# A hybrid RG-LRU and attention layer: the fourth column tile of xr takes block 0 of x with the first three, and the LRU work stands one step later

## Chip, core and metric

The kernel runs on one core of one Trainium2 chip. The metric is the device time of one execution in microseconds (us). Engines are named as in the profile: PE does the matmuls, PEld loads their weights, DVE is the vector engine, ACT the scalar engine, POOL is GpSimd, SP only issues DMAs here. L435 is line 435 of the kernel before the change.

## What is computed

One layer of an encoder trunk on x of 512 positions by 1024 channels, in float32:

```
h = RMSNorm(x)
[xr | gate | q | k | v] = h @ W_in                  # 512, 512, 512, 512, 512 columns
xr = depthwise conv of width 4 over positions
h_f, h_b = forward and backward RG-LRU of xr        # r, i = sigmoid gates of xr, block by block
y_rnn = (h_f + h_b) * gelu(gate)
y_attn = dilated attention of q, k, v, 8 heads, with a T5 bias by relative position
x = x + concat(RMSNorm(y_rnn), RMSNorm(y_attn)) @ W_out
x = x + relu(RMSNorm(x) @ W_up)^2 @ W_down
out = RMSNorm(x)
```

In the RG-LRU, a = exp(c r) and b = sqrt(1 - a^2) * i * xr feed a scan over the positions, one forward and one backward.

## The kernel before

**Precision.** Every float32 operand is split into two parts (hi on ACT by a copy to the matmul type, lo on DVE by subtracting hi), and each product is three matmuls: hi·hi, hi·lo and lo·hi, done by mm3 (L303 to L305). Weights come in chunks of 128x1024. For chunk i, conv_hi(i) makes whi (L251 on ACT, L249 on DVE for chunks 7, 8 and 9), and conv_lo(i) makes wlo on DVE (L259). conv_lo also issues the load of a later chunk into the buffer that it has read.

**Order.** PE, ACT, DVE and POOL run their instructions in the order in which the program's text emits them, so an instruction that waits holds all that stand behind it on its engine. DMAs issued by ACT (L468) and POOL stand in those orders too. SP issues the other DMAs.

**The head.** x comes transposed in eight blocks k of 128 channels; each comes with the 3x128 weight columns of column tiles 0 to 2 of xr for that block (L325 to L328). cvx(k) (L336) makes h_hi and h_lo of the block (x times the norm's gain; the row factor rstd is applied later) and splits its weights. sq(k) squares x for the norm. PE adds up pxr[0..2] over k as the blocks come (L431 to L438). Within the last block it also transposes the sum of squares (turned, L422, the tile pcs). From pcs come the row sums on DVE (L427), rcol on POOL (a power, L403), and by a PE transpose (prow, L395) and an ACT copy the tile rstd (rrow, L409). The fourth column tile pxr[3] uses chunk 3, a whole 128x1024 chunk loaded after the blocks, and is computed afterwards by xmm (L648), in pieces before and after prow.

**conv and LRU.** conv_a(t) multiplies pxr[t] by rstd (DVE L486) and starts the conv on ACT (L488). conv_b(t) adds its other three taps on DVE (L493 to L495). POOL meanwhile runs a softplus polynomial (L161 to L173, some twenty tiny operations) that starts from a DVE result emitted behind conv_a(1) (L159, L160) and whose last results scale the exponentials. Behind it POOL issues the load of the bias rows (relt, L664).

**V and gate.** The loop over 32 steps n for V (L695) makes one mm3 per step, about 0.68 us, and one over 32 steps of the gate projection follows (L734). Other work is hung on step numbers: GATES says at which n lru_gates(t) puts 8 small matmuls (pg, L514) and their sigmoids (ga, L517). lru_hooks(n) hands out lru_x (DVE L522), lru_exp (ACT L531, L532), lru_sqrt (ACT L537), and, at the numbers in SC, the 16 pieces of the scans (DVE L548, L549, L555, L557). bias_round(0) at n = 7 is the first user of relt on DVE (L454). bias_prep at n = 20 is two matmuls, two DVE negations (nbs, L467) and two DMAs issued by ACT (L468); it stands behind lru_hooks(20) in that step, so behind lru_exp(2) and the first scan piece.

**Into attention.** 16 steps of K and Q of head pair 0 follow. k_evac (kraw, L750) and q_evac (qraw, L746) read PSUM on DVE. s_hi (ACT L757) and s_lo (DVE L766 for K, L769 for Q) split the results, and att_s (PE L782, L783) forms the scores ps. A dictionary plan says which extra work stands at which point of the attention loop; rnn_end(t) is two DVE operations (L582, L583) that add the two scans and multiply by the gate, and rnn_end(0) stands at point (0, 0, 0), just after the first scores.

Of the kernel before, what the change touches and what calls it, by code (L numbers as in the profile page):

```python
# [14 lines left out]
AF = mybir.ActivationFunctionType  # L15
OP = mybir.AluOpType

P = 128
S = 512
D = 1024  # L20
KD = D // P
# [80 lines left out]
def hybrid_kernel(ctx: ExitStack, tc, xw0, xw, xn, w_in, w_v, w_out, w_up, w_dn, gates, vecs, rel, onehot, fg, out):  # L102
    nc = tc.nc
# [8 lines left out]
    act = nc.scalar.activation  # L112
# [3 lines left out]
    def g_(name, dt=FT, shape=(P, S)):  # L116
        return work.tile(list(shape), dt, name=name, tag="g", bufs=NG)
# [4 lines left out]
    def ps_(name, tag):  # L122
        return psum.tile([P, S], FT, name=name, tag=tag, bufs={"pj": 4, "gs": 2, "et": 2}[tag])

    def f(t):
        return t.bitcast(FT)
# [175 lines left out]
    def mm3(o, a, b, first, last, on=False):  # L302
        nc.tensor.matmul(o, lhsT=a[0], rhs=b[0], start=bool(first), stop=False, skip_group_check=on)  # L303
        nc.tensor.matmul(o, lhsT=a[0], rhs=b[1], start=False, stop=False, skip_group_check=on)  # L304
        nc.tensor.matmul(o, lhsT=a[1], rhs=b[0], start=False, stop=bool(last), skip_group_check=on)  # L305
# [13 lines left out]
    for k in range(KD):  # L319
        if 4 <= k < 7:  # L320
            xwt.append(stream.tile([P, 1024], FT, name="wraw", tag="wraw", bufs=3)[:, :XW])
        else:
            xwt.append(work.tile([P, 1024], FT, name="tw", tag="tw", bufs=4)[:, :XW if k else XG + 3 * P])
        if k == 0:
            nc.sync.dma_start(xwt[0][:, :XG], xw0[:, :XG])  # L325
            nc.sync.dma_start(xwt[0][:, XG:], xw0[:, XG:])
        else:
            nc.sync.dma_start(xwt[k], xw[k - 1])  # L328
        if k == 6:
            nc.sync.dma_start(vt, vecs)  # L330
# [5 lines left out]
    def cvx(k):  # L336
        x, w = xwt[k][:, :S], xwt[k][:, S if k else XG:]
        g = ag[:, k:k + 1] if k else xwt[0][:, S:S + 1]
        hi, lo = g_("w3h", FR), g_("w3l", FR)
        if k < 2:  # L340
            c = (2 * P, 3 * P)[k]
            act(h_hi[:, k, :c], x[:, :c], AF.Copy, scale=g)
            nc.vector.tensor_scalar(h_hi[:, k, c:], x[:, c:], g, None, op0=OP.mult)
            if k == 0:
                nc.vector.tensor_copy(hi[:, :2 * P], w[:, :2 * P])
                act(hi[:, 2 * P:3 * P], w[:, 2 * P:], AF.Copy)
            else:
                nc.vector.tensor_copy(hi[:, :3 * P], w)
        else:
            act(h_hi[:, k, :], x, AF.Copy, scale=g)  # L350
            act(hi[:, :3 * P], w, AF.Copy)
        stt(h_lo[:, k, :], x, g, f(h_hi)[:, k, :], op0=OP.mult, op1=OP.subtract)
        nc.vector.tensor_tensor(lo[:, :3 * P], w, f(hi)[:, :3 * P], op=OP.subtract)
        w3.append((hi, lo))

    def sq(k):
# [22 lines left out]
    def hk(k):  # L379
        return (h_hi[:, k, :], h_lo[:, k, :])  # L380

    def wk(c, k):
        if c < 3:
            return tuple(t[:, c * P:(c + 1) * P] for t in w3[k])
        hi, lo = splits[c]
        return (hi[:, k * P:(k + 1) * P], lo[:, k * P:(k + 1) * P])
# [19 lines left out]
    def row_tile(cols, tag):  # L406
        pr = rows_of(lambda tt: fan(cols, tt, 1, P), tag)
        r = g_("rrow")
        act(r, pr, AF.Copy)  # L409
        return r  # L410
# [8 lines left out]
    def turned(ss, tag):  # L419
        pc = ps_("pcs", tag)  # L420
        for tt in range(4):
            nc.tensor.transpose(pc[:, tt * P:(tt + 1) * P], ss[:, tt * P:(tt + 1) * P], ident)  # L422
        return pc
# [3 lines left out]
        nc.vector.tensor_reduce(c, pc.rearrange("p (t c) -> p t c", t=4), axis=mybir.AxisListType.X, op=OP.add)  # L427
        return c

    pxr = {t: ps_("pxr", "pj") for t in range(3)}  # L430
    for k in range(KD):  # L431
        if k < 2:
            for i, (a, b) in enumerate(((0, 0), (0, 1), (1, 0))):
                for t in range(3):
                    nc.tensor.matmul(pxr[t], lhsT=wk(t, k)[a], rhs=hk(k)[b], start=i == 0 and k == 0, stop=False)  # L435
            continue
        for t in range(3):
            mm3(pxr[t], wk(t, k), hk(k), False, k == KD - 1)  # L438
            if k == KD - 1 and t == 0:
                sqt = turned(sqx[0], "et")  # L440


# [41 lines left out]
    def conv_a(t, pp):  # L484
        xr = g_("xr")
        nc.vector.tensor_tensor(xr, pp, rstd, op=OP.mult)  # L486
        c = g_("xc")
        act(c, xr, AF.Identity, scale=vec("w2", t), bias=vec("cb", t))  # L488
        xrt[t], xc[t] = xr, c

    def conv_b(t):
        xr, c = xrt.pop(t), xc[t]
        stt(c[:, 2:], xr[:, :S - 2], vec("w0", t), c[:, 2:], op0=OP.mult, op1=OP.add)  # L493
        stt(c[:, 1:], xr[:, :S - 1], vec("w1", t), c[:, 1:], op0=OP.mult, op1=OP.add)
        stt(c[:, :S - 1], xr[:, 1:], vec("w3", t), c[:, :S - 1], op0=OP.mult, op1=OP.add)  # L495
        xcs[t] = swapped("xcs", c)
# [22 lines left out]
    def lru_x(t):  # L519
        for m, x in ((1, xc[t]), (3, xcs.pop(t))):  # L520
            o = gact[t, m]
            nc.vector.tensor_tensor(o, o, x, op=OP.mult)  # L522
        del gwr[t], xc[t]
# [3 lines left out]
    def lru_exp(t):  # L527
        for d in range(2):
            r = gact[t, 2 * d]
            a = g_("la")  # L530
            act(a, r, AF.Exp, scale=cneg[:, d * 4 + t:d * 4 + t + 1])  # L531
            act(r, r, AF.Tanh, scale=chalf[:, d * 4 + t:d * 4 + t + 1])  # L532
            lru_a[t, d] = a
# [5 lines left out]
    def lru_gelu(t):  # L539
        act(gt[t], gt[t], AF.Gelu_apprx_tanh)  # L540
# [102 lines left out]
                sub.popleft()()  # L643


    pxr[3] = ps_("pxr", "pj")

    def xmm(ks):  # L648
        for k in ks:
            mm3(pxr[3], wk(3, k), hk(k), k == 0, k == KD - 1)  # L650

    for i in (3, 4, 5):
        conv_hi(i)
# [1 line left out]
    rcol = rstd_cols(row_sums(sqt), D)  # L655
    for i in (4, 5):
        conv_lo(i)
    xmm((0, 1, 2))
    rstd = row_tile(rcol, "et")
    conv_a(0, pxr[0])  # L660
    conv_a(1, pxr[1])
# [2 lines left out]
    nc.gpsimd.dma_start(relt, rel)  # L664
    for i in range(2):
        nc.gpsimd.dma_start(oht[i], onehot[:, i * S:(i + 1) * S])
    xmm((3, 4))
    conv_b(0)
    act(warm, epsb, AF.Sigmoid)
    conv_a(2, pxr[2])  # L670
    xmm((5, 6, 7))
    conv_a(3, pxr[3])
    conv_hi(6)
    conv_b(1)
# [4 lines left out]
    def lru_hooks(n):  # L679
        if n in (9, 10, 13, 14):  # L680
            lru_x({9: 0, 10: 1, 13: 2, 14: 3}[n])
        if n in (13, 14, 20, 21):
            lru_exp({13: 0, 14: 1, 20: 2, 21: 3}[n])
        if n in (17, 19, 28, 29):
            t = {17: 0, 19: 1, 28: 2, 29: 3}[n]
            lru_sqrt(t)
            scans.extend(scan_ops(t)[:4])
        if n in SC:
            scans.popleft()()

    GATES = {2: 0, 5: 1, 8: 2, 11: 3}
    pv = {}
    vtag = {0: "et", 2: "gs", 3: "gs", 1: "et"}
    steps = [(k, tt) for k in range(KD) for tt in (0, 2, 3, 1)]
    for n, (k, tt) in enumerate(steps):  # L695
        c = C_V + k // 2
        if k == 0:
            pv[tt] = ps_("pv", vtag[tt])
        hi, lo = splits[c]
        sl = slice((k % 2) * S, (k % 2 + 1) * S)  # L700
        tsl = slice(tt * P, (tt + 1) * P)
        mm3(pv[tt], (h_hi[:, k, tsl], h_lo[:, k, tsl]), (hi[:, sl], lo[:, sl]), k == 0, k == KD - 1)
        if n >= 16:
            feed(c, n % 8)
        if n in GATES:
            lru_gates(GATES[n])
        if n == 2:
            conv_b(2)
        if n == 6:
            conv_b(3)  # L710
            conv_lo(6)
        if n == 7:
            conv_hi(7)
            conv_lo(7)
        if n in (7, 9):
            bias_round((n - 7) // 2)
        if n == 12:
            conv_hi(8)
            conv_lo(8)
        lru_hooks(n)  # L720
        if n == 20:
            bias_prep()
            load_tw(0)
            load_tw(1)
    vs = big.tile([P, 4, S], FT, name="vs", tag="bigC")
    last = [scan_ops_end(t) for t in range(4)]
# [6 lines left out]
    gsteps = [th for t in range(4) for th in proj_thunks(C_G + t, "pj", gate_done(t))]  # L733
    for n, th in enumerate(gsteps):  # L734
        th()
        lru_hooks(32 + n)
        if n in (19, 21, 27, 29):
            tt = {19: 0, 21: 2, 27: 3, 29: 1}[n]
            act(vs[:, tt, :], pv[tt], AF.Copy, scale=rcol[:, tt:tt + 1])
# [191 lines left out]
    def wo_thunks():  # L931
# [17 lines left out]
            return run  # L949
        return [mk(b, *o) for b, o in enumerate(order)]  # L950

    KSPLIT = {7: s_hi, 8: s_lo}
    for n, th in enumerate(q_thunks(0, 1) + q_thunks(0, 0)):
        th()
        if n in KSPLIT:
            for e in range(2):
                KSPLIT[n](0, 1, e)
        if n % 4 == 0:
            lru_gelu(n // 4)
    fillers = deque()  # L960

    def fill(n):
# [22 lines left out]
            for b in bs[1:]:  # L985
                nc.gpsimd.dma_start(t, oblock(b), accum_op=OP.add)

    def rnn_end(t):
        last[t]()

    def rnn_sq(t):
        y_sq(yrnn[t], 0)

# [6 lines left out]
    def end(t):  # L1000
        return lambda: rnn_end(t)

    def sq_(t):
        return lambda: rnn_sq(t)
# [4 lines left out]
    def op(fn, *a):  # L1009
        return lambda: fn(*a)  # L1010


    plan = {(0, 0, 0): [end(0)], (0, 0, 2): [sq_(0), add], (0, 0, 3): [end(1)],
            (0, 1, 1): [sq_(1)],
            (0, 2, 3): [add],
            (1, 0, 2): [end(2)],
# [138 lines left out]
    for w in OSEQ:  # L1155
        for i in range(4):
            tt, k = i // 2, i % 2
# [550 lines left out]
```

## Time and profile before

| | |
|---|---|
| median of 3 runs | 540.1 us (539.34 to 540.29) |
| the profiled execution, its own time | 539.75 us |
| its span, first to last instruction | 538.0 us |
| time around the span | 1.75 us |
| granted PE clock, mean | 0.997 |
| instructions | 8174 |

The profile shows one execution. A row of its timeline gives start and duration in us, the engine and line, output <- inputs, a shape, how many instructions are merged (x2), and in brackets how long the engine had been idle before and what ended that. A merged row's duration covers all its instructions; neighbours overlap by about 0.1 us, since an engine starts the next instruction while the last one drains. A matmul row of 0.39 us is one of a pipelined stream in which the next starts 0.23 us later. PE and DVE rows are therefore compared by their starts.

### The profile page before, as it was taken

What the parts mean: (1) busy time and instruction counts of PE and PEld (TensorE: products, weight loads), DVE (VectorE), ACT (ScalarE), POOL (GpSimd) and SP (SyncE); (2) the same over time, 40 slices, a digit from 0 to 9 for tenths busy, and PEclk for the clock granted to TensorE, in tenths of its full rate; (3) what the DMA queues carried; (4) which work ended last, traced back from release to release, by engine and by line L of the source; (5) the groups of instructions that cost most, each with busy time, mean ns of one, the idle gap of its engine ahead of it and who ended that gap; (6) DMA issues with size and microseconds to landing.
All of it is one profiled execution on the core that took longest, in us unless ns stands there. A gap on an engine that the chain in (4) does not pass through costs nothing.

```text
span 538.0 us, 8174 instructions
## 1 busy us (share of the span) xinstructions
PE 530.2 (99%) x3007; PEld 450.3 (84%) x3007; DVE 433.7 (81%) x636; ACT 362.3 (67%) x574; POOL 67.5 (13%) x92
## 2 busy tenths in 40 slices
PE   9999999999999999999999999999999999999995
PEld 7857888886886578889999888888999999888884
DVE  6895998996863689889769987879756987987885
ACT  6678955898865746586566755566657686755664
POOL 0182000000001131001030223001101210131000
PEclk9999999999999999999999999999999999999998
DMA  7743385465499788856586799994887496799704
GB/s 276 246 110 109 111 274 185 130 184 158 117 361 239 163 161 231 285 188 176 175 171 179 193 252 275 288 358 115 282 236 200 130 218 185 173 290 262 190 1 157
DMA packets 36664, 108.00 MB, mean 201 GB/s; under 512 B 4484, under 2 KB 7556, under 8 KB 36624
## 3 DMA queue, kind: packets, MB, share of 16 engines
q1 hardware_dynamic: 28480, 78.49, 42.5%
q0 software_dynamic: 7968, 28.76, 28.5%
q8 instruction: 23, 0.38, 0.3%
q10 hardware_dynamic: 176, 0.23, 0.1%
q14 instruction: 17, 0.14, 0.1%
HBM read 98.00 MB, written 4.23 MB: 190 GB/s over the span
## 4 chain that ended last, share of the span: by engine, by line
PE 98%; DVE 0%; issue 0%; DVEq 0%; ACT 0%; ACTq 0%
PE pu L303 10%; PE pu L305 10%; PE pu L304 10%; PE pd L305 9%; PE pd L303 9%; PE pd L304 9%; PE pqk L303 3%; PE pwo L303 3%; PE pqk L304 3%; PE pqk L305 3%; PE pav L897 3%; PE pt L806 3%; PE pwo L305 3%; PE pwo L304 3%; PE pv L303 2%; PE pp L305 1%
## 5 line engine op out<-in xcount | busy, mean ns | idle before, releaser
L259 DVE TENSOR_TENSOR wlo<-wraw,whi 128x1024 fp32r<-128x1024 f32 x73 | 88.9, 1220 | 20.5 <-ACT whi L251 20.2
L251 ACT ACTIVATE whi<-wraw 128x1024 fp32r<-128x1024 f32 x70 | 74.1, 1060 | 36.2 <-PE pd L305 18.8
L304 PE MATMUL pd<-wlo,ah 128*128 128x512 f32 (+1 forms) x195 | 75.2, 386 | 0.0
L303 PE MATMUL pd<-whi,ah 128*128 128x512 f32 (+1 forms) x195 | 75.2, 386 | 0.0
L305 PE MATMUL pd<-whi,al 128*128 128x512 f32 (+1 forms) x195 | 75.2, 386 | 0.0
L304 PE MATMUL pu<-hl,whi 128*128 128x256 f32 x224 | 63.4, 283 | 0.0
L305 PE MATMUL pu<-hh,wlo 128*128 128x256 f32 x224 | 63.4, 283 | 0.0
L303 PE MATMUL pu<-hh,whi 128*128 128x256 f32 x224 | 63.4, 283 | 0.0
L251 ACT ACTIVATE whi<-tw 128x1024 fp32r<-128x1024 f32 x36 | 38.1, 1060 | 33.8 <-PE pu L304 10.0
L303 PE MATMUL pu<-h2h,whi 128*128 128x256 f32 (+1 forms) x200 | 60.1, 300 | 0.0
L304 PE MATMUL pu<-h2l,whi 128*128 128x256 f32 (+1 forms) x200 | 60.0, 300 | 0.0
L305 PE MATMUL pu<-h2h,wlo 128*128 128x256 f32 (+1 forms) x200 | 60.0, 300 | 0.0
L259 DVE TENSOR_TENSOR wlo<-tw,whi 128x1024 fp32r<-128x1024 f32 x36 | 44.0, 1222 | 16.6 <-ACT whi L251 16.3
L304 PEld LDWEIGHTS pu<-hl,whi 128*128 128x128 f32 x224 | 43.0, 192 | 0.0
L303 PEld LDWEIGHTS pu<-hh,whi 128*128 128x128 f32 x224 | 43.0, 192 | 0.0
L305 PEld LDWEIGHTS pu<-hh,wlo 128*128 128x128 f32 x224 | 43.0, 192 | 0.0
L304 PEld LDWEIGHTS pd<-wlo,ah 128*128 128x128 f32 x195 | 36.6, 188 | 7.4
L305 PEld LDWEIGHTS pd<-whi,al 128*128 128x128 f32 x195 | 36.6, 188 | 7.3
L303 PEld LDWEIGHTS pd<-whi,ah 128*128 128x128 f32 x195 | 36.6, 188 | 7.3
L251 ACT ACTIVATE whi<-ts 128x1024 fp32r<-128x1024 f32 x24 | 25.5, 1061 | 25.4 <-PE pd L305 18.1
L305 PEld LDWEIGHTS pu<-h2h,wlo 128*128 128x128 f32 x200 | 38.3, 191 | 1.3
L304 PEld LDWEIGHTS pu<-h2l,whi 128*128 128x128 f32 x200 | 38.3, 191 | 1.3
(278 smaller groups left out, 1259.5 us busy)
## 6 DMA issues: line engine op xcount, KB each, us to landing
wraw<-in_w_up_dram SPq DMA_DIRECT2D x25, 512.0 KB, 3.6
ts<-in_w_dn_dram POOLq DMA_DIRECT2D x24, 512.0 KB, 13.7
wraw<-in_w_dn_dram SPq DMA_DIRECT2D x24, 512.0 KB, 9.4
tw<-in_w_up_dram SPq DMA_DIRECT2D x15, 512.0 KB, 9.4
tw<-in_w_up_dram POOLq DMA_DIRECT2D x15, 512.0 KB, 7.3
wraw<-in_w_in_dram SPq DMA_DIRECT2D x13, 512.0 KB, 4.2
ts<-in_w_dn_dram SPq DMA_DIRECT2D x8, 512.0 KB, 4.6
tw<-in_w_dn_dram SPq DMA_DIRECT2D x8, 512.0 KB, 8.8
```

The source lines that it names most:

```text
L251: act(hi, raws[i], AF.Copy)
L259: nc.vector.tensor_tensor(lo, r, f(splits[i][0]), op=OP.subtract)
L303: nc.tensor.matmul(o, lhsT=a[0], rhs=b[0], start=bool(first), stop=False, skip_group_check=on)
L304: nc.tensor.matmul(o, lhsT=a[0], rhs=b[1], start=False, stop=False, skip_group_check=on)
L305: nc.tensor.matmul(o, lhsT=a[1], rhs=b[0], start=False, stop=bool(last), skip_group_check=on)
L806: nc.tensor.transpose(pt[:, qt * P:(qt + 1) * P], en[h][qt][:, jt * P:(jt + 1) * P], ident)
L897: nc.tensor.matmul(pav[p][a, :], lhsT=vs[:, jt, h * DH:(h + 1) * DH], rhs=et.pop((h, jt)), start=jt == 0, stop=jt == 3)
```

## The change

The fourth column tile's weights for block 0 come by a small DMA of their own (128 rows of 512 bytes, w03) right behind block 0. They are split on ACT and DVE within cvx(0), and pxr[3] gets its three matmuls for block 0 with the first three tiles. The transposes for pcs stand behind column tile 1 of the last block, not 0. The remaining seven blocks of pxr[3] come as four before prow and three behind (before: three and five).

Within V, the LRU gates stand one step later (GATES), lru_hooks too, in V and in the gate projection, and so do conv_b(2) and conv_b(3). bias_round, bias_prep and the conversions of chunks stay at their numbers. rnn_end(0) moves from point (0, 0, 0) of the attention loop to step 9 of the K and Q projections, behind the split of K.

```diff
         if k == 0:
             nc.sync.dma_start(xwt[0][:, :XG], xw0[:, :XG])
             nc.sync.dma_start(xwt[0][:, XG:], xw0[:, XG:])
+            w03 = g_("w03")[:, :P]
+            nc.sync.dma_start(w03, w_in[3][:, :P])
...
         nc.vector.tensor_tensor(lo[:, :3 * P], w, f(hi)[:, :3 * P], op=OP.subtract)
+        if k == 0:
+            act(hi[:, 3 * P:], w03, AF.Copy)
+            nc.vector.tensor_tensor(lo[:, 3 * P:], w03, f(hi)[:, 3 * P:], op=OP.subtract)
...
-        if c < 3:
+        if c < 3 or (c, k) == (3, 0):
             return tuple(t[:, c * P:(c + 1) * P] for t in w3[k])
...
+            if k == 0:
+                mm3(pxr[3], wk(3, 0), hk(0), True, False)
             continue
...
-            if k == KD - 1 and t == 0:
+            if k == KD - 1 and t == 1:
                 sqt = turned(sqx[0], "et")
...
-    xmm((0, 1, 2))
+    xmm((1, 2, 3, 4))
     rstd = row_tile(rcol, "et")
...
-    xmm((3, 4))
+    xmm((5, 6))
     conv_b(0)
...
-    xmm((5, 6, 7))
+    xmm((7,))
...
-    GATES = {2: 0, 5: 1, 8: 2, 11: 3}
+    GATES = {3: 0, 6: 1, 9: 2, 12: 3}
...
-        if n == 2:
+        if n == 3:
             conv_b(2)
-        if n == 6:
+        if n == 7:
             conv_b(3)
...
-        lru_hooks(n)
+        lru_hooks(n - 1)
         if n == 20:
             bias_prep()
...
-        lru_hooks(32 + n)
+        lru_hooks(32 + n - 1)
...
         if n % 4 == 0:
             lru_gelu(n // 4)
+        if n in [9]:
+            rnn_end([9].index(n))
...
-    plan = {(0, 0, 0): [end(0)], (0, 0, 2): [sq_(0), add], (0, 0, 3): [end(1)],
+    plan = {(0, 0, 2): [sq_(0), add], (0, 0, 3): [end(1)],
```

More of the change, by code (lines that the diff above doesn't have):

```diff
@@ L428, in row_sums @@
         return c
-    pxr = {t: ps_("pxr", "pj") for t in range(3)}
+    pxr = {t: ps_("pxr", "pj") for t in range(4)}
     for k in range(KD):
@@ L643, in weave @@
                 sub.popleft()()
-    pxr[3] = ps_("pxr", "pj")
     def xmm(ks):
         for k in ks:
-            mm3(pxr[3], wk(3, k), hk(k), k == 0, k == KD - 1)
+            mm3(pxr[3], wk(3, k), hk(k), False, k == KD - 1)
     for i in (3, 4, 5):
@@ L950, in wo_thunks, with rnn_end @@
         return [mk(b, *o) for b, o in enumerate(order)]
+    def rnn_end(t):
+        last[t]()
     KSPLIT = {7: s_hi, 8: s_lo}
@@ L986, in load_x @@
                 nc.gpsimd.dma_start(t, oblock(b), accum_op=OP.add)
-    def rnn_end(t):
-        last[t]()
     def rnn_sq(t):
```

## The prediction

> **What bounds the kernel now.** I read the page first: busy shares, then the chain of waits that ended last; then the busy time by stretches.
>
> ```profile
> PE 530.2 (99%) x3007; PEld 450.3 (84%) x3007; DVE 433.7 (81%) x636; ACT 362.3 (67%) x574; POOL 67.5 (13%) x92
> PE 98%; DVE 0%; issue 0%; DVEq 0%; ACT 0%; ACTq 0%
> ```
>
> ```profile
> 60.00:75.00 15.00, 14.98 (x66) 12.07 (x65) 14.73 (x18) 10.25 (x14) 0.00 (x0) 1.00 0.59 171
> 75.00:90.00 15.00, 15.00 (x68) 12.43 (x67) 14.17 (x18) 8.52 (x12) 0.00 (x0) 1.00 0.65 216
> ```
>
> PE is busy for 99% of the span, and 98% of the chain lies on it. The change removes no matmul, so it wins only where PE waits today and loses wherever PE comes to wait. The last two rows (stretch, length, then busy us of PE, PEld, DVE, ACT, POOL) show the danger: from 60 to 90 us DVE works 14.73 and 14.17 of 15 us. What comes late on DVE there stays late.
>
> **Step 1: the head gains 0.38 us.** PE's timeline; each row from 7.33 on begins a group of nine matmuls, those of one block for tiles 0 to 2:
>
> ```profile
> 4.48 1.57 PE L435 MATMUL pxr<-h_hi,w3h 128*128 128x512 f32 x3
> 5.89 0.85 PE L435 MATMUL pxr<-h_lo,w3h 128*128 128x512 f32 x3
> ...
> 7.33 0.93 PE L435 MATMUL pxr<-h_hi,w3h 128*128 128x512 f32 x3
> ...
> 9.58 0.39 PE L303 MATMUL pxr<-h_hi,w3h 128*128 128x512 f32 x1
> ...
> 11.81 0.39 PE L303 MATMUL pxr<-h_hi,w3h 128*128 128x512 f32 x1
> ...
> 13.86 0.39 PE L303 MATMUL pxr<-h_hi,w3h 128*128 128x512 f32 x1
> ```
>
> Block 3 takes 13.86 - 11.81 = 2.05 us, 0.228 a matmul; block 1 takes 2.25 and block 2 takes 2.23. So PE waits 0.20 + 0.18 = 0.38 us for its data. Three more matmuls at block 0 (3 x 0.228 = 0.68 us) push blocks 1 and 2 behind their data and fill those waits. Behind block 2 PE is 0.68 - 0.38 = 0.30 us late; once the three are missing from xmm, it is 0.38 early.
>
> What w03 itself adds, by rows of SP, ACT and DVE:
>
> ```profile
> 1.17 0.42 SPq L326 DMA_DIRECT2D tw<-in_xw_dram  x1
> ```
>
> ```profile
> 3.91 0.31 ACT L346 ACTIVATE w3h<-tw 128x128 fp32r<-128x128 f32 x1
> ...
> 6.62 0.62 ACT L342 ACTIVATE h_hi<-tw,ag 128x384 fp32r<-128x384 f32 x1 [1.88 <-DMA tw<-in_xw_dram]
> ```
>
> ```profile
> 6.63 0.28 DVE L343 TENSOR_SCALAR h_hi<-tw,ag 128x128 fp32r<-128x128 f32 x1 [1.30 <-DMA tw<-in_xw_dram]
> ```
>
> One more issue on SP is 0.42 us, one more copy on ACT 0.31, one more 128x128 operation on DVE about 0.28. ACT idles 1.88 us and DVE 1.30 us at that place, so both operations are hidden if w03 has landed by about 5.7. The DMA issued at 1.17 was used by 3.91, and w03 is issued 0.46 us after it. The later blocks land between 0 and 0.42 us later (no row has a 64 KB load here). PE asks for block 1 about 0.6 us later than now, so I take 0 and keep the 0.42 for the range.
>
> **Step 2: rstd, and all vector work behind it, comes 0.98 us later.** Rows of PE, DVE and POOL:
>
> ```profile
> 20.66 0.60 PE L422 MATMUL pcs<-ident,sqx 128*128 128x128 f32 x4
> ...
> 30.55 1.95 PE L514 MATMUL pg<-xc,gwr 64*64 64x512 f32 x16
> ```
>
> ```profile
> 21.30 0.68 DVE L427 TENSOR_REDUCE cs<-pcs 128x4 f32<-128x512 f32 x1
> ...
> 28.96 0.75 DVE L495 SCALAR_TENSOR_TENSOR xc<-xr,vt,xc 128x511 f32<-128x511 f32 x1
> ...
> 46.49 0.23 DVE L454 CAST relr<-relt 97x128 fp32r<-97x128 f32 x1 [5.88 <-DMA relt<-in_rel_dram]
> ```
>
> ```profile
> 27.56 0.64 POOL L161 TENSOR_TENSOR z<-z,e 128x8 f32<-128x8 f32 x1 [3.33 <-DVE z L160]
> ...
> 42.58 0.84 POOL L664 DMA_DIRECT2D relt<-in_rel_dram  x1
> ```
>
> pcs stands behind one more group of three, so it comes 0.30 + 0.68 = 0.98 us later, and the reduce follows it at once today (20.66 + 0.60 = 21.26). As many matmuls as before, 15, stand between pcs and prow, so prow, rstd and conv_a(0) also come 0.98 later. Behind conv_a(1) on DVE stands the result that POOL waits for at 27.56; POOL then needs 15.0 us before it issues relt. DVE waits 5.88 us for relt, and from 46.49 on works almost without a gap. So the whole stretch starts 0.98 us later, although PE in V is 0.38 early. The LRU gates fit: one step later (0.68) less 0.38 puts them 0.30 later on PE, their conv inputs 0.98 later; today xc(0) is ready at 28.96 + 0.75 = 29.71 and used at 30.55, a margin of 0.84 that covers the 0.68.
>
> **Step 3: ACT is held by its own DMA issues.** Rows of ACT, then of DVE:
>
> ```profile
> 54.80 2.20 ACT L537 ACTIVATE ga<-ga 128x512 f32<-128x512 f32 x4
> 57.01 1.28 ACT L531 ACT_TABLE_LOAD   x1
> 58.31 0.73 ACT L531 ACTIVATE la<-ga,cneg 128x512 f32<-128x512 f32 x1
> ...
> 60.50 0.92 ACTq L468 DMA_DIRECT2D nbd<-nbs  x2
> 61.46 0.72 ACT L531 ACTIVATE la<-ga,cneg 128x512 f32<-128x512 f32 x1 [0.30 <-DMA nbd<-nbs]
> ...
> 64.22 1.05 ACT L251 ACTIVATE whi<-wraw 128x1024 fp32r<-128x1024 f32 x1
> ...
> 68.68 1.99 ACT L251 ACTIVATE whi<-wraw 128x1024 fp32r<-128x1024 f32 x2
> ```
>
> ```profile
> 57.99 0.69 DVE L548 SCALAR_TENSOR_TENSOR ga<-la,ga 128x512 f32<-128x512 f32 x1
> ...
> 59.32 1.27 DVE L467 TENSOR_SCALAR nbs<-pbias 8x512 f32<-8x512 f32 x2
> ...
> 68.20 1.22 DVE L557 TENSOR_TENSOR_SCAN ga<-la,ga 128x512 f32<-128x512 f32 x1
> 69.34 2.33 DVE L259 TENSOR_TENSOR wlo<-wraw,whi 128x1024 fp32r<-128x1024 f32 x2
> ...
> 88.55 0.68 DVE L750 TENSOR_TENSOR kraw<-pqk,rrow 128x512 f32<-128x512 f32 x1
> ...
> 92.19 1.23 DVE L259 TENSOR_TENSOR wlo<-wraw,whi 128x1024 fp32r<-128x1024 f32 x1 [0.85 <-ACT whi L251]
> ...
> 94.71 1.40 DVE L769 TENSOR_TENSOR qs<-qraw,qs 64x512 fp32r<-64x512 f32 x2 [0.70 <-ACT qs L757]
> ...
> 98.81 0.69 DVE L582 TENSOR_TENSOR ga<-ga,hs 128x512 f32<-128x512 f32 x1
> ...
> 100.14 0.68 DVE L750 TENSOR_TENSOR kraw<-pqk,rrow 128x512 f32<-128x512 f32 x1
> ```
>
> Today lru_exp(2) stands ahead of the two nbd issues on ACT and fills the time until nbs exists; only 0.30 us is lost. bias_prep keeps step 20 while lru_exp(2) moves to step 21, so the issues now come first, straight behind the square roots, and behind them wait eight exponentials and tanhs, then whi of chunks 10 and 11. nbs moves ahead of the first scan piece: 57.99 + 0.98 = 58.97, both done 1.27 later at 60.24. ACT is free at 57.00 + 0.30 = 57.30 and stands. The second issue (0.46) ends at 60.73; table load 1.28 + 0.02: exponentials at 62.03 instead of 58.31. whi10 starts 64.22 - 58.31 - 0.30 = 5.61 later, 67.64; whi11 starts 68.68 - 64.22 = 4.46 behind it, 72.10, and ends at 73.15. On DVE, wlo11 (the second of 69.34) starts at 70.45 today and would be due at 71.43; it now waits until 73.18: **2.73 us late**. wlo10 is served first, since the scan at 68.20 has moved behind it: it ends at 69.18 + 1.22 = 70.40.
>
> The Trainium skill (ScalarE: Activation LUTs, What ACT_TABLE_LOAD costs) puts a switch at about 2.66 us, a 1.28 us load and a 1.38 us drain. By that price the sum would be 1.4 us higher; the rows here have 0.02 us between load and first use and 0.01 ahead of the load, so I take the rows.
>
> **Step 4: the scores wait.** From wlo11 to kraw DVE has no gap, so kraw comes at 91.28. rnn_end(0) costs 100.14 - 98.81 = 1.33 us in the place where DVE waits 0.85 today: 0.48 more. qs is finished at 94.71 + 1.41 = 96.12 today, at 96.12 + 2.73 + 0.48 = 99.33 then. PE's rows:
>
> ```profile
> 70.59 0.50 PE L305 MATMUL pp<-h_hi,wlo 128*128 128x512 f32 x1
> ```
>
> ```profile
> 96.16 0.39 PE L782 MATMUL ps<-kh,qs 128*128 128x512 f32 x1
> ...
> 96.61 0.39 PE L782 MATMUL ps<-kh,qs 128*128 128x512 f32 x1
> ```
>
> The matmul at 70.59 uses wlo10 and starts 0.03 behind its end; at 70.43 then, PE has 0.16 of its 0.38 left. The second head's scores start at 96.61 today, 0.5 behind qs. They start at 99.38: **2.8 us later**, with PE idle 2.9. Behind them PE runs without waits of note, while DVE has 1.33 us less to do, so little is taken back; I allow 0.1.
>
> **Sum.** -0.16 + 2.9 - 0.1 = +2.6 to 2.7 on the profiled execution's own 539.75 us (span 538.0 and 1.75 around it): **542.4 us**. That execution lies within the three runs shown, 0.35 under their median.
>
> **Rivals.**
> - **ACT isn't held** (the issues wait apart from its arithmetic). For it: the 0.92 us of issues cost it only 0.30. Against: that row shows ACT idle until the second issue was out. Then qs is late by 0.98 + 0.48 = 1.46, the scores start at 97.63: +1.0, **540.8**.
> - **No measurable change: POOL's chain gets shorter.** Place: 27.56 to 42.58, the 15.0 us of step 2. If relt came 3 us sooner than I say, nbs would be there when ACT comes free; whi11 would end at 70.64 (57.30 + 0.92 + 1.30 puts the exponentials at 59.52), wlo11 be 0.22 late, qs 0.70, the scores +0.3: **540.0**. It decides from 1.7 us of shortening (2.8 less 1.1, which is 0.2%). Against: DVE's work beside the chain shifts with it.
> - **w03 lands late.** At 7.0, ACT's copy (0.31) and square (about 0.62, as the row at 6.62) and then h_hi (0.62) end at 8.55 instead of 7.24; 1.3 less the room of 0.6 is 0.7 more: **543.1**.
> - **The clock falls in the 2.9 us wait.** The first three matmuls took 5.89 - 4.48 = 1.41 us where three take 0.68 later: PE starts slow. If the wait brought that back, as much again is lost, 0.73: **543.1**. The Trainium skill (TensorE: Matmul & The Clock Gate, What's actually happening) has the clock halve after an idle window of about 3.4 us; by that rule 2.9 us would mostly not do it, and no wait that long stands in this trace behind the start.
>
> **How the numbers follow.** The forecast has 0.58 (541.8 to 543.2 by itself), ACT not held 0.14, the shorter chain 0.12, late w03 and the clock together 0.08 (543.1). No row supports a gain beyond 0.2%; 0.08 stay for what I can't see, 0.05 of them faster. A difference under 0.2% (1.1 us) can't be told from none. Slower: 0.58 + 0.08 + half of 0.14 + 0.01 = 0.74; same 0.12 + 0.07 + 0.02 = 0.21; faster 0.05. The range of 8 in 10 goes from the shorter chain's 540.0 to 543.5, past late w03.
>
> **What would show it.** Right: blocks 1 and 2 of pxr at 2.05 us each; relr near 47.5; ACT idle from about 57.3 until the nbd issues; DVE idle before wlo11 for 1.7 us; a PE wait of 2 to 3 us at L782. Wrong: relr at 46 or earlier, exponentials at 58 to 60, or scores without a wait.

## The result and the profile after

| | before | after |
|---|---|---|
| median of 6 runs each, us | 539.75 (539.05 to 540.29) | 543.3 (542.34 to 544.61) |
| profiled execution, span, us | 538.0 | 541.3 |
| granted PE clock, mean | 0.997 | 0.994 |

The ratio after to before is 1.0061, with a 95% interval of 1.0046 to 1.0075. By the medians the change costs 3.55 us, by the ratio 3.3. Line numbers behind L325 have moved by up to 7 in the changed kernel.

PE's share fell from 99% to 98%, and the chain of waits is no longer PE's alone (page, after):

```profile
span 541.3 us, 8174 instructions
PE 531.2 (98%) x3007; PEld 451.6 (83%) x3007; DVE 434.8 (80%) x637; ACT 362.7 (67%) x575; POOL 67.7 (12%) x92
PE 85%; DVE 6%; ACT 3%; POOL 3%; issue 2%; DMA 1%; ACTq 0%; DVEq 0%; POOLq 0%
```

PE's timeline, after. First the head, where the rows at 7.82, 9.86 and 11.90 begin blocks 1, 2 and 3 for tiles 0 to 2; then the place of the first scores, and the row in which the next step's scores begin:

```profile
7.82 0.84 PE L440 MATMUL pxr<-h_hi,w3h 128*128 128x512 f32 x3
...
9.86 0.39 PE L303 MATMUL pxr<-h_hi,w3h 128*128 128x512 f32 x1
...
11.90 0.39 PE L303 MATMUL pxr<-h_hi,w3h 128*128 128x512 f32 x1
...
95.28 0.39 PE L305 MATMUL pqk<-h_hi,wlo 128*128 128x512 f32 x1
98.20 0.80 PE L787 MATMUL ps<-kh,qs 128*128 128x512 f32 x1 [2.53 <-DVE qs L774]
98.79 0.63 PE L788 MATMUL ps<-kl,qs 128*128 128x512 f32 x1
99.21 0.63 PE L787 MATMUL ps<-kh,qs 128*128 128x512 f32 x1
...
100.49 0.63 PE L304 MATMUL pqk<-h_lo,whi 128*128 128x512 f32 x1
100.92 0.47 PE L305 MATMUL pqk<-h_hi,wlo 128*128 128x512 f32 x1
101.23 0.39 PE L303 MATMUL pqk<-h_hi,whi 128*128 128x512 f32 x1
...
103.30 0.39 PE L787 MATMUL ps<-kh,qs 128*128 128x512 f32 x1
```

Block 1 takes 9.86 - 7.82 = 2.04 us and block 2 11.90 - 9.86 = 2.04: the waits of the head are gone. PE finishes its work ahead of the scores at 95.28 + 0.23 = 95.51, earlier than before (95.93 + 0.23 = 96.16), and then stands until 98.20: **2.69 us**. Behind that, most matmuls start some 0.42 us apart instead of 0.23 until 101. The stretches show why (length, busy us of PE, PEld, DVE, ACT, POOL, then the granted clock):

```profile
95.50:98.20 2.70, 0.17 (x2) 0.01 (x1) 1.97 (x4) 1.36 (x3) 0.00 (x0) 0.90 0.58 169
98.20:101.00 2.80, 2.80 (x7) 2.20 (x8) 2.47 (x5) 2.24 (x2) 0.00 (x0) 0.50 0.19 79
101.00:104.00 3.00, 3.00 (x15) 2.47 (x14) 2.47 (x7) 2.92 (x7) 0.00 (x0) 0.99 0.58 180
```

From 98.20 to 101.00 the granted clock is 0.50. It fell while PE still stood: a mean of 0.90 over the 2.70 us from 95.50 on means some 0.5 us at 0.50, so the fall comes near 97.7. It is back just behind 101.0, as the 0.99 of the next stretch says. The low clock lasted about 3.4 us.

ACT's timeline, after:

```profile
55.16 2.19 ACT L544 ACTIVATE ga<-ga 128x512 f32<-128x512 f32 x4
59.16 0.93 ACTq L475 DMA_DIRECT2D nbd<-nbs  x2
60.12 1.28 ACT L538 ACT_TABLE_LOAD   x1 [2.77 <-DVE nbs L474]
61.42 0.72 ACT L538 ACTIVATE la<-ga,cneg 128x512 f32<-128x512 f32 x1
```

The square roots end at 57.35, and ACT computes nothing for 2.77 us: it stands until DVE's nbs lets the two issues go at 59.16, and the issues take until 60.09. DVE's timeline, after:

```profile
22.06 0.69 DVE L432 TENSOR_REDUCE cs<-pcs 128x4 f32<-128x512 f32 x1 [1.07 <-PE pcs L427]
...
46.91 0.23 DVE L461 CAST relr<-relt 97x128 fp32r<-97x128 f32 x1 [5.55 <-DMA relt<-in_rel_dram]
...
58.46 1.27 DVE L474 TENSOR_SCALAR nbs<-pbias 8x512 f32<-8x512 f32 x2
...
68.68 1.22 DVE L259 TENSOR_TENSOR wlo<-wraw,whi 128x1024 fp32r<-128x1024 f32 x1
69.81 1.22 DVE L564 TENSOR_TENSOR_SCAN ga<-la,ga 128x512 f32<-128x512 f32 x1
72.45 1.23 DVE L259 TENSOR_TENSOR wlo<-wraw,whi 128x1024 fp32r<-128x1024 f32 x1 [1.42 <-ACT whi L251]
...
90.79 0.68 DVE L755 TENSOR_TENSOR kraw<-pqk,rrow 128x512 f32<-128x512 f32 x1
...
97.46 1.41 DVE L774 TENSOR_TENSOR qs<-qraw,qs 64x512 fp32r<-64x512 f32 x2 [0.69 <-ACT qs L762]
```

relr is 0.42 us later than before, wlo of chunk 11 waits 1.42 us for its whi, kraw is 2.24 late (90.79 against 88.55), qs 2.75 (97.46 against 94.71).

### The profile page after: what moved, and what is told of

It is laid out like the page before. It is cut to its first block, busy times and chain, and to the rows that moved or that the text cites. A ratio compares the mean times of both kernels' runs of the same rounds, so it can differ in the third digit from the quotient of the medians.

```text
span 541.3 us, 8174 instructions
## 1 busy us (share of the span) xinstructions
PE 531.2 (98%) x3007; PEld 451.6 (83%) x3007; DVE 434.8 (80%) x637; ACT 362.7 (67%) x575; POOL 67.7 (12%) x92
## 3 DMA queue, kind: packets, MB, share of 16 engines
HBM read 98.06 MB, written 4.23 MB: 189 GB/s over the span
## 4 chain that ended last, share of the span: by engine, by line
PE 85%; DVE 6%; ACT 3%; POOL 3%; issue 2%; DMA 1%; ACTq 0%; DVEq 0%; POOLq 0%
PE pu L304 10%; PE pu L305 10%; PE pu L303 10%; PE pd L303 9%; PE pd L304 9%; PE pd L305 9%; PE pwo L303 3%; PE pav L902 3%; PE pt L811 3%; PE pwo L305 3%; PE pwo L304 3%; PE pqk L303 2%; PE pqk L304 2%; PE pqk L305 2%; DVE wlo L259 2%
## 5 line engine op out<-in xcount | busy, mean ns | idle before, releaser
L303 PEld LDWEIGHTS pu<-h2h,whi 128*128 128x128 f32 x200 | 38.3, 191 | 1.3
```

## Experiments

**Theory A** is the prediction's: rstd late, ACT held by its own DMA issues, the moved sum; they add up on DVE, and PE stands at the first scores. Seeing the profile after, I added a fourth piece, the low clock that came with that wait. **Rival B**: the head with its small DMA costs the time. **Rival C**: ACT's idle time costs nothing, since late rstd and the sum hold DVE by themselves. Each experiment is set against runs of the kernel before that were made beside it: 539.90 us for e1 to e4, 539.76 for c and e5 to e7, 540.17 for e8 to e10.

**e1: the issues behind lru_exp(2) again.** The edit moves the whole of bias_prep by a step, with its matmuls and nbs, and two loads by SP that stand behind it.

```diff
-        if n == 20:
+        if n == 21:
             bias_prep()
```

> The changed kernel with bias_prep one step later, at 21, so that its two DMA issues stand behind lru_exp(2) on ACT again. Theory (ACT held by its own DMA issues): in the changed kernel wlo of chunk 11 waits 1.42 us for whi, and that wait goes; qs ends about 1.4 us sooner, the scores wait under 1.5 us instead of 2.9, and the slow stretch of PE behind the wait goes too: 540.5 to 541.3 us against 543.3 for the changed kernel. Rival (the late rstd and the moved sum alone hold DVE): no idle time of DVE matters, 543.3 stays within 0.5.

540.49 us against 539.90 (ratio 1.0014, 1.0002 to 1.0025). DVE, e1:

```profile
47.34 0.23 DVE L461 CAST relr<-relt 97x128 fp32r<-97x128 f32 x1 [5.88 <-DMA relt<-in_rel_dram]
...
71.19 1.20 DVE L259 TENSOR_TENSOR wlo<-wraw,whi 128x1024 fp32r<-128x1024 f32 x1
...
96.18 1.40 DVE L774 TENSOR_TENSOR qs<-qraw,qs 64x512 fp32r<-64x512 f32 x2 [0.70 <-ACT qs L762]
```

wlo of chunk 11 no longer waits. relr is later than in the changed kernel's trace (47.34 against 46.91), yet qs is 1.28 earlier. One step number takes away some 2.5 us (0.0061 - 0.0014 = 0.0047 of 540) of the change's cost, or 3.0 by the medians; C falls.

**e2: the sum back at its old point.**

```diff
-        if n in [9]:
-            rnn_end([9].index(n))
...
-    plan = {(0, 0, 2): [sq_(0), add],
+    plan = {(0, 0, 0): [end(0)], (0, 0, 2): [sq_(0), add],
```

> The changed kernel with rnn_end(0) back at point (0, 0, 0), behind the first scores. Theory: qs ends 0.5 us sooner (97.46 + 1.41 becomes 98.4), so the wait for the scores falls from 2.9 to 2.4 us: 542.8, or 542.0 if the shorter wait also spares PE the slow matmuls behind it. Rival (the sum is what holds Q back): over 2 us less, 541 or under.

543.09 us (1.0054, 1.0038 to 1.0070), 0.3 above the expected 542.8, which can't be told from the changed kernel. In its trace relr comes at 48.07 by itself, so this one execution can't be compared by its clock times. What can be compared is the interval from relr to qs, since DVE works through between them:

| kernel | relr | qs | relr to qs | PE stands before the scores | median, us (before, run beside it) |
|---|---|---|---|---|---|
| before | 46.49 | 94.71 | 48.22 | 0 | 539.75 |
| after | 46.91 | 97.46 | 50.55 | 2.69 | 543.3 (539.75) |
| c, after once more | 47.28 | 97.75 | 50.47 | 2.70 | 544.02 (539.76) |
| e1, issues behind | 47.34 | 96.18 | 48.84 | 1.22 | 540.49 (539.90) |
| e2, sum back | 48.07 | 98.06 | 49.99 | 2.21 | 543.09 (539.90) |
| e4, hooks and sum back | 49.74 | 97.95 | 48.21 | 0 | 540.71 (539.90) |
| e6, before with later hooks | 47.49 | 97.46 | 49.97 | 2.17 | 542.14 (539.76) |
| e7, issues behind, sum back | 47.61 | 95.96 | 48.35 | 0.70 | 540.51 (539.76) |

The held ACT is worth 49.99 - 48.22 = 1.77 us of this interval, the sum 48.84 - 48.22 = 0.62; together 2.39, and 50.55 - 48.22 = 2.33 is measured. e3 and e5, which change nothing ahead of the scores, have 50.50 and 50.65. The column on PE leaves out what PE waited earlier, for wlo10: 0.6 us in e2 and 1.9 in e4.

**e4: hooks and sum at their old places.** The changed kernel with the edit of e2 and

```diff
-        lru_hooks(n - 1)
+        lru_hooks(n)
...
-        lru_hooks(32 + n - 1)
+        lru_hooks(32 + n)
```

> The changed kernel with lru_hooks at its old numbers and rnn_end(0) at its old point: what is left is the head with w03 and the gates and conv_b one step later. Theory: rstd is 0.75 us late and the bias rows 0.4, wlo10 stands behind its scan again and PE waits for it about 0.9 us where it waits 0.2 before the change; qs is 0.4 late: 539.9 to 540.3 against 539.75 for the kernel before. Rival (the head with its small DMA is what costs): 542 or more.

540.71 us (1.0019, 1.0002 to 1.0036). It is a little over the expected range and under 542: B falls. The head with the later gates costs 0.8 us by the medians, and at most 1.9 by the interval. The traced execution also had block 2 of x late (PE began it at 10.51, against 9.86), and PE waited 1.90 us for wlo10, so the order that the old hooks give (wlo10 behind its scan) does bear on a late DVE, more than I had put down.

**c: the changed kernel again, beside e5 to e7.**

> The changed kernel itself, as it is, beside the others of this call. Both theories expect 543.3 us again (542.9 to 543.7), and in its trace 2.3 us more from the first use of the bias rows on DVE (relr) to qs than the 48.2 us of the kernel before.

544.02 us (1.0073, 1.0059 to 1.0087), 0.3 above the expected 543.7; the interval from relr to qs is as expected. In the traced execution the wait was as long (2.70), but the clock stayed at 1.00; it took 542.46 us. c's stretches and PE rows, then one row of PE before:

```profile
95.80:98.50 2.70, 0.16 (x2) 0.02 (x1) 1.97 (x4) 1.37 (x3) 0.00 (x0) 1.00 0.53 137
98.50:101.00 2.50, 2.50 (x10) 1.77 (x11) 2.17 (x3) 2.23 (x2) 0.00 (x0) 1.00 0.28 113
```

```profile
98.49 0.50 PE L787 MATMUL ps<-kh,qs 128*128 128x512 f32 x1 [2.54 <-DVE qs L774]
...
102.52 0.39 PE L787 MATMUL ps<-kh,qs 128*128 128x512 f32 x1
```

```profile
99.78 0.39 PE L782 MATMUL ps<-kh,qs 128*128 128x512 f32 x1
```

From the first scores to the next step's scores PE runs 16 matmuls. They take 99.78 - 96.16 = 3.62 us before, 102.52 - 98.49 = 4.03 in c, and 103.30 - 98.20 = 5.10 in the first trace of the changed kernel. So the low clock cost 1.07 us there. The other 0.41 us is lost at full clock: in c the score matmuls start 0.33 to 0.38 us apart. e1, e2, e5 and e7 show it too, and e3, where PE didn't stand; its cause stays open.

**e3 and e5: PE kept busy in the wait.** 11, then 6 matmuls whose result nobody reads:

```diff
+            if i == 0 and u == 0:
+                pf = ps_("pfill", "et")
+                for _ in range(11):
+                    nc.tensor.matmul(pf, lhsT=h_hi[:, 0, :P], rhs=h_hi[:, 0, :], start=True, stop=True)
             if i < 4:
                 att_s(i, u)
```

> The changed kernel with 11 matmuls of 512 columns (h_hi with itself into a tile that nobody reads; 2.5 us) ahead of the first scores, where PE waits 2.9 us anyway. Theory (PE's clock falls in the wait, 0.50 granted from 98.2 to 101, 7 matmuls at 0.42 instead of 0.23): the fill costs nothing and keeps the clock, 0.7 to 0.9 us less than the changed kernel, 542.4 to 542.6. Rival (the slow matmuls come from something else, such as late data or a busy memory): they stay slow, 543.3, or more by what the fill overruns.

> The changed kernel with 6 idle matmuls (1.4 us) in place of the 11 ahead of the first scores, too short to hold the scores back. Theory (PE's clock falls in the wait and the slow matmuls behind it are part of the loss): no matmul at 0.42 us behind the wait, and 0.5 to 0.9 us less than the changed kernel in this call. Rival (the slow matmuls are seen but their time is lost to the data anyway, since DVE and ACT still come late): no difference, as with 11.

e3: 543.33 us (1.0055, 1.0040 to 1.0070), where 542.4 to 542.6 was expected, so no gain in time was measured. e5: 543.12 (1.0067, 1.0054 to 1.0080), 0.9 under c, but the two intervals overlap. The granted clock tells more than the times: over the 11 runs of the changed kernel (after and c) the mean clock is 0.994 in 8 and 0.997 in 3; over the 11 runs with a fill it is 0.996 to 0.998 in all. So work in the wait keeps the clock up. The medians of those 8 and those 3 are 543.8 and 542.5, a difference of about 1.3 us, near the 1.07 of the rows above. But the 11 runs with a fill have a median of 543.2, not 542.5. That the fill pays in time isn't shown, and where its gain goes stays open.

**e6: the hooks alone, on the kernel before.** The two edits of lru_hooks from the change, nothing else.

> The kernel before with lru_hooks one step later and nothing else. Theory (ACT held by its DMA issues): 1.7 to 1.8 us more from relr to qs, as in the trace of the run with the sum put back; the scores wait 1.3 us or more, 541.0 to 541.5. Rival (the head is needed for the loss): 539.8 to 540.2, as before.

542.14 us (1.0040, 1.0024 to 1.0055): more than expected, and without any of the head. ACT, e6:

```profile
59.69 0.91 ACTq L468 DMA_DIRECT2D nbd<-nbs  x2
60.62 1.28 ACT L531 ACT_TABLE_LOAD   x1 [3.48 <-DVE nbs L467]
```

Here ACT is idle 3.48 us, and the clock falls too, though PE stood only 2.17 us; the fall comes 1 us after PE resumed and the low clock again lasts 3.4 us. e6's stretches:

```profile
98.20:99.20 1.00, 1.00 (x3) 0.57 (x4) 0.67 (x1) 0.98 (x2) 0.00 (x0) 1.00 0.73 287
99.20:102.60 3.40, 3.40 (x9) 2.66 (x9) 3.36 (x7) 2.79 (x5) 0.00 (x0) 0.50 0.34 107
```

Its 16 matmuls from 98.20 on take 5.63 us, 1.60 more than in c. The three runs with a mean clock of 0.997 or more took 540.64 to 541.62 us, close to what was expected; the three with 0.995 or 0.996 took 542.66 to 543.00.

**e7: issues behind and sum back.** The edits of e1 and e2 together.

> The changed kernel with bias_prep at step 21 and rnn_end(0) back at its old point: the head and the later LRU are left. Theory: 48.2 us from relr to qs, as before; only the late rstd is left, which puts qs 0.4 to 1.2 us late against PE 0.7 early: 539.9 to 540.4. Rival (a part of the loss that is in none of the three): 541 or more.

540.51 us (1.0014, 1.0003 to 1.0025), 0.1 over the expected range. The interval is 48.35, as before; what is left is the late start: relr at 47.61, and PE stands 0.70 us.

**e8 to e10: the bias rows loaded early.** POOL issues relt and oht right behind rcol:

```diff
     rcol = rstd_cols(row_sums(sqt), D)
+    nc.gpsimd.dma_start(relt, rel)
+    for i in range(2):
+        nc.gpsimd.dma_start(oht[i], onehot[:, i * S:(i + 1) * S])
...
     cneg, chalf = next(spc)
-    nc.gpsimd.dma_start(relt, rel)
-    for i in range(2):
-        nc.gpsimd.dma_start(oht[i], onehot[:, i * S:(i + 1) * S])
```

e8 is the changed kernel with this edit, e9 is e7 with it, e10 the kernel before with it.

> The changed kernel with the three loads of the bias rows (relt and oht) issued by POOL right behind rcol instead of behind the softplus. Theory (DVE's crowded stretch starts when relt has landed, and everything late in it is late for that): relr comes at 41 to 42 us instead of 47, nbs exists when ACT comes free, so ACT is held only for the two issues (0.9 us), and qs is less than 1 us late: 539.6 to 540.5 against 543.3 to 544.0. Rival (ACT's order alone decides): the issues still stand ahead of lru_exp(2), 542 or more.

> The same early loads, with bias_prep at step 21 and rnn_end(0) at its old point: the head with w03 and the later LRU are left. Theory: neither wlo10 nor qs holds PE, so the 0.4 us of the head and the 0.3 us of wlo10 are kept: 538.9 to 539.4 against 539.76 to 539.9 for the kernel before. Rival (the bias rows' loads collide with the weights' loads at 25 us): V's weights come late and PE waits in V, 540 or more.

> The kernel before with the early loads of the bias rows and nothing else. Theory: DVE has 4 us to spare from 46 us on, PE no longer waits for wlo10 (0.3 us), and the runs spread less, since the landing of the bias rows no longer decides: 539.2 to 539.6. Rival (these loads collide): 540 or more.

Against 540.17 us for the kernel before: e8 539.36 (0.9986, 0.9977 to 0.9994), e9 539.46 (0.9990, 0.9981 to 0.9999), e10 539.42 (0.9985, 0.9976 to 0.9995). All three are 0.7 to 0.8 us under the kernel before and can't be told from one another, so that gain is the early loads' and not the change's. e8 is below its expected range, e9 0.06 above, e10 within; but e10's runs don't spread less than those of the kernel before (538.65 to 541.24, against 538.98 to 541.21). DVE, e8:

```profile
40.81 0.23 DVE L461 CAST relr<-relt 97x128 fp32r<-97x128 f32 x1
...
52.33 1.27 DVE L474 TENSOR_SCALAR nbs<-pbias 8x512 f32<-8x512 f32 x2
...
69.25 1.23 DVE L259 TENSOR_TENSOR wlo<-wraw,whi 128x1024 fp32r<-128x1024 f32 x1 [2.09 <-ACT whi L251]
...
94.27 1.40 DVE L774 TENSOR_TENSOR qs<-qraw,qs 64x512 fp32r<-64x512 f32 x2 [0.70 <-ACT qs L762]
```

relr starts with no wait, nbs exists 3 us before ACT's square roots end, so the issues go out during these (at 54.77 and 55.41) and cost ACT nothing, and qs is earlier than in the kernel before. wlo of chunk 11 waits 2.09 us for its whi even here, but DVE is so far ahead that this holds nobody. Against e10 the whole change then costs nothing, and its gains at the head and at wlo10 (0.4 and 0.3 us) don't show in the time either.

## Why the prediction was right, and where it was not

- **Step 1 (head, 0.38 us saved): right.** Block 1 takes 2.04 us; w03 was in use on ACT at 5.12, before 5.7. With PE at 95.51 instead of 96.16 ahead of the scores, 0.65 us were saved in all (0.37 in c), but only to stand.
- **Step 2 (all vector work 0.98 late): right in kind, too large in this execution.** The reduce came 0.76 late, since block 0 took 7.12 - 4.47 = 2.65 us instead of 7.33 - 4.48 = 2.85. The issue of relt was 0.76 late too (43.34), relr 0.42. From issue to use relt took 3.57 us here, 3.91 before, and 3.28 to 5.24 over the traces of c and e1 to e7. The forecast carried the delay over as if this time were fixed; it scatters by 2 us, more than the 1.75 forecast for the hold.
- **Step 3 (ACT held; wlo11 2.73 late): right.** ACT's idle time ended by nbs is there, and wlo11 is 2.00 late: 0.42 from relr, and by subtraction 1.58 from the hold. Predicted for the hold was 2.73 - 0.98 = 1.75; e2 and e6 give 1.77 and 1.75 of the interval.
- **Step 4 (sum 0.48; scores 2.8 late): right.** e1 gives 0.62. The second head's scores start at 99.21, 2.60 late, but some 0.3 of that is the low clock: qs is finished at 97.46 + 1.41 = 98.87, and in c, at full clock, these scores start 0.05 behind qs (99.20). c's are 2.59 late by qs alone.
- **What the sum lacked: the clock.** I priced it as a rival at 0.73 us, added to the forecast, and gave it 0.08 with another case. The price came from the kernel's first three matmuls, where the profile grants 1.00 (4 to 6 us), so those rows don't show a low clock. It occurred in 8 of 11 runs of the changed kernel, by their mean clock, and cost 1.07 us in the trace. c's traced execution, without it, took 542.46, and 542.4 was forecast. So it can make up the 0.9 us between forecast and median, 543.3; the runs with a fill, at 543.2, keep this from being shown. That the forecast misses the first traced execution (543.1) by only 0.7 is partly luck: relr was 0.98 - 0.42 = 0.56 us less late than forecast, and the clock took that back and more. The Trainium skill (TensorE: Matmul & The Clock Gate, What's actually happening) has the clock fall after an idle window of about 3.4 us. By that I had left it out for a wait of 2.9 us; here the clock fell to 0.50 with waits of 2.69 and 2.17 us, and not with one of 2.70. The same section calls the window free-running, which fits a fall in some runs and not in others. Both low stretches lasted about 3.4 us; where such a window begins, no run here shows.
- **Rival "ACT isn't held": wrong**, as ACT's rows show. **Rival "no measurable change by a shorter POOL chain"**: the chain kept its length (43.34 - 28.30 = 15.04 us by POOL's rows, 15.02 before), but its mechanism is what e8 shows: with relt early, the loss is gone.

## What to carry to other kernels

Here a DMA issued by ACT was an instruction in ACT's order, and its wait became ACT's. When work is shifted by a step, look at what the shift leaves standing in front of such an issue and whether its data is there yet. Where one engine is crowded for 40 us, ask what its first instruction waits for, and move that, not the work behind it. And compare two traces by an interval between two instructions of the crowded engine, which scatters less than the times themselves: over the traces of the changed kernel, c, e3 and e5, relr moved by 2 us and the interval by 0.2.

## What the runs showed of the hardware

- PE's granted clock fell to 0.50 in two traces in which PE had stood for less than 3 us: some 2.2 us into a wait of 2.69 (after: 95.51 to 97.7), and 1 us behind the end of a wait of 2.17 (e6). Each low stretch lasted about 3.4 us. Waits of 2.70 us (c) and 2.21 us (e2) were not followed by one.
- From issue to first use, a 48.5 KB load issued by POOL took 3.3 to 5.2 us over ten traces that load it at the same point of the program.
- Two DMAs issued by ACT ahead of their data left ACT idle for 2.77 us (after) and 3.48 us (e6); with exponentials in front of them, 0.30 us (before).
